# Taps of a causal convolution pinned to their place in the source, and a lighter gate for gated attention, in a one-core decoder layer

## The chip, the cores and the metric

The kernel runs on one core of a Trainium2 chip. The metric is the device time in microseconds of one execution, taken as the median of several. The engines are named as in the profile: PE (TensorE matmul, with PEld for its weight loads), DVE (VectorE), ACT (ScalarE), POOL (GpSimd) and SP (SyncE, which only issues transfers here). Each has its own queue and works through it strictly in order.

## The reference

One layer over 256 tokens of width 2048. The input is projected into four groups of mixers; their outputs are scaled, projected by `w_out`, added and normalized; then comes a mixture of 32 experts and a second normalization. What the change touches lies in the first part:

```python
u = x @ w_in[i]
a_u, gq, gk, gv, g_low, g_r, cq, ck, cv, sb, sc, sh = jnp.split(u, split_idx, axis=-1)
y_a = conformer_conv(a_u, ...)   # h = a * sigmoid(gate); causal depthwise conv of 31 taps; LayerNorm; silu
y_b = gla_mixer(gq, gk, gv, g_low, g_r, w_g2, b_g2, norm_g)
y_c = dilated_mixer(cq, ck, cv, rel_bias)
y_d = short_gated_conv(sb, sc, sh, conv_w)
...
# in gla_mixer, 8 chunks of 32 tokens:
log_a = log_sigmoid(g_low @ w_g2 + b_g2) / 16
b = cumsum(log_a within a chunk)          # then exp(b), exp(b - b_mid), exp(b_last - b) scale q and k
```

## The kernel before

The first 400 us are one long row of projections: eleven blocks of 512 columns of `w_in` (in order cg, ca, v, qk, r, cq, ck, cv, sc, sh, sb) and then `w_out` (wo). Each block has 16 steps, one for 128 rows of the weights. To get float32 accuracy from a faster format, a step splits its weights in two: `split` (L249) lets ACT round them to `wh` (L253), and then DVE or POOL subtracts to get the rest, `wl` (L256). A counter `nsplit` decides which: of three splits in a row, two are DVE's and the third POOL's. PE then does three kinds of matmul for each quarter of the block: `wh` with the rounded input `xh` (L276), `wh` with the input's rest `xl` (L277), `wl` with `xh` (L278); twelve matmuls a step. In the blocks v and cv (L295 to L297) the roles of weights and inputs are swapped and there are six wider matmuls a step. The pool of staged halves has 8 buffers, so four pairs of `wh` and `wl`.

Between the steps `pump` lets generators do the rest of the work in small pieces. `tasks` come first, and `behind` is served only when no task is left. `conv` (L320, in `behind`) computes the 31-tap convolution on DVE: for each of four channel blocks `cb` a first multiplication (L323) and then 30 taps (L325), each adding a shifted, scaled copy of `hp` to `ya`, with a yield after every second tap; then its LayerNorm with sums over PE, and `silu`. `gla_gate` (L398, a task during qk) turns the projected gate into the factors `e12`, `e34` and `dec`; `gla_state` (during r) computes the attention's states, `gla_out` (during cq) its output. `attention` and `sconv` run during sc, sh and sb.

The code gives the data flow; the order in which an engine's queue holds its instructions is chosen by a list scheduler with its own model of durations. It may hold back or bring forward everything that no data ties down. After the first 400 us comes the routing and the mixture of experts, whose order on PE is written out by hand and which the change does not touch.

Of the kernel before, what the change touches and what calls it, by code (L numbers as in the profile page):

```python
# [12 lines left out]
AF = mybir.ActivationFunctionType  # L13
ALU = mybir.AluOpType
# [5 lines left out]
P = 128  # L20
T = 256
# [103 lines left out]
def trunk(ctx, tc, where, vecs_d, lasting, early, gla, xT, x, pT_d, w_in, w_out, ple_w_gate, exp_w_gu, exp_w_down, ple_w_proj, out):  # L125
    nc = tc.nc
    V, S, G, PE = nc.vector, nc.scalar, nc.gpsimd, nc.tensor
# [14 lines left out]
    def bank(name="bank", tag="mx", bufs=None):  # L142
        return pp.tile([P, 512], F32, name=name, tag=tag, bufs=bufs)

    def work(shape, dt=F32, name="w"):
        return wk.tile(shape, dt, name=name, tag="w")

    def stage(shape, dt=F32R, name="st"):
        return st.tile(shape, dt, name=name, tag="st")
# [4 lines left out]
    def f32(ap):  # L154
        return ap.bitcast(F32)
# [8 lines left out]
    def const(name, r=P, t=None):  # L164
        a, n = (at_l if t is None else t)[name]
        return {id(None): cl, id(at_e): ce, id(at_g): cg_}[id(t)][0:r, a:a + n]

    def col(name, i=0):
        a = at_l[name][0] + i
        return cl[:, a:a + 1]  # L170

    def dww(k, cb):
        i = k * 4 + cb
        return const("conf_dw_w", t=at_e)[:, i:i + 1]
# [37 lines left out]
    def quarter(q, part, shape=None, name="mix"):  # L212
        return qm.tile(shape or [P, 4, T], F32 if shape else F32R, name=name, tag=f"q{q}{part}")
# [5 lines left out]
    nsplit = [0]  # L219
    debt = [0]  # L220

    def pump(n=1):

        debt[0] = debt[0] + n if tasks or behind else 0
        while debt[0] >= 1 and (tasks or behind):
            q = tasks or behind
            try:
                next(q[0])
                debt[0] -= 1
            except StopIteration:  # L230
                q.pop(0)
        if not (tasks or behind):
            debt[0] = 0

    def drain():
        while tasks:
            pump()

    def load_half(w, name, sizes=(4, 4), before=None):

        s = slot([P, 8, 512], name)
        a = 0
        for n in sizes:
            if before is not None:
                before(a, a + n)
            nc.sync.dma_start(s[:, a:a + n], w[:, a:a + n])
            a += n
        return s

    def split(w):  # L250
        wh = stage([P, w.shape[1]], F32R, "wh")
        wl = stage([P, w.shape[1]], F32R, "wl")
        S.copy(wh, w)  # L253
        e = G if nsplit[0] % 3 == 2 else V
        nsplit[0] += 1
        e.tensor_sub(wl, w, f32(wh))  # L256
        return wh, wl

    def first_half(k, w, name):
        s = load_half(w, name, (4, 4) if k else (1, 1, 2, 4), lambda a, b: load_x(slice(k + a, k + b)))  # L260
        if k:
            small_loads()
        return s

    def proj_ch(name, rate=1, first=False):

        w = w_in[list(BLOCKS).index(name)]
        bs = [bank(name + "0", "ps"), bank(name + "1", "ps")]
        for k in range(KT):
            if k % 8 == 0:  # L270
                s = first_half(k, w[k // 8], name + "w") if first else load_half(w[k // 8], name + "w")
            wh, wl = split(s[:, k % 8, :])
            for cb in range(4):
                o = bs[cb // 2][:, (cb % 2) * T:(cb % 2 + 1) * T]
                h, l = wh[:, cb * P:(cb + 1) * P], wl[:, cb * P:(cb + 1) * P]
                PE.matmul(o, h, xh[:, k, :], start=(k == 0 and cb % 2 == 0), stop=False, skip_group_check=True)  # L276
                PE.matmul(o, h, xl[:, k, :], start=False, stop=False, skip_group_check=True)  # L277
                PE.matmul(o, l, xh[:, k, :], start=False, stop=(k == KT - 1), skip_group_check=True)  # L278
            pump(rate)
        return [bs[cb // 2][:, (cb % 2) * T:(cb % 2 + 1) * T] for cb in range(4)]  # L280
# [20 lines left out]
    def put_mix(kt, y):  # L301

        q, a = kt // 4, kt % 4
        if (q, "h") not in mix:
            mix[q, "h"], mix[q, "l"] = quarter(q, "h"), quarter(q, "l")
        h = mix[q, "h"][:, a:a + y.shape[1], :]
        S.copy(h, y)
        V.tensor_sub(mix[q, "l"][:, a:a + y.shape[1], :], y, f32(h))
# [7 lines left out]
    hp = quarter(0, "l", [P, 4, T], "hp")  # L316
# [3 lines left out]
    def conv():  # L320
        ya = quarter(3, "h", [P, 4, T], "ya")
        for cb in range(4):
            V.tensor_scalar(ya[:, cb, :], hp[:, cb, :], dww(30, cb), const("conf_dw_b", t=at_e)[:, cb:cb + 1], op0=ALU.mult, op1=ALU.add)  # L323
            for d in range(1, 31):
                V.scalar_tensor_tensor(ya[:, cb, d:T], hp[:, cb, 0:T - d], dww(30 - d, cb), ya[:, cb, d:T],  # L325
                                       op0=ALU.mult, op1=ALU.add)
                if d % 2 == 0:
                    yield
        def total(v):
            u = work([P, 2, T], name="u")  # L330
            V.tensor_add(u, v[:, 0:2], v[:, 2:4])
            V.tensor_add(u[:, 0], u[:, 0], u[:, 1])
            return u[:, 0]

        u = total(ya)
        yield
        b = bank("mu")
        PE.matmul(b[:, 0:T], ones, u, start=True, stop=True)
        V.scalar_tensor_tensor(ya, b[:, None, 0:T].to_broadcast([P, 4, T]), -1.0 / 512, ya, op0=ALU.mult, op1=ALU.add)
        yield  # L340
        sq = work([P, 4, T], name="sq")
        S.activation(sq, ya, AF.Square)
        u = total(sq)
        yield
        b = bank("var")
        PE.matmul(b[:, 0:T], ones, u, start=True, stop=True)
        yield
        rs = work([P, 2, T], name="rs")
        S.activation(rs[:, 0], b[:, 0:T], AF.Sqrt, scale=1.0 / 512, bias=eps_ln[:, 0:1])
        V.reciprocal(rs[:, 1], rs[:, 0])  # L350
        yield
        V.tensor_mul(ya, ya, rs[:, 1:2, :].to_broadcast([P, 4, T]))
        yield
        for cb in range(4):
            S.activation(ya[:, cb, :], ya[:, cb, :], AF.Silu, scale=col("conf_ln_g", cb), bias=col("conf_ln_b", cb))
            V.tensor_scalar_mul(ya[:, cb, :], ya[:, cb, :], col("mix_scale", cb))
            yield
        for cb in range(4):
            put_mix(cb, ya[:, cb:cb + 1, :])
            yield  # L360
# [30 lines left out]
    e12 = work([P, 2, 2, T], name="e12")  # L391
    e34 = work([P, 2, 2, T], name="e34")
# [5 lines left out]
    def gla_gate():  # L398
        zb = bank("z")
        for blk in range(2):  # L400
            PE.matmul(zb[:, blk * T:(blk + 1) * T], const("wg2", P, at_g)[:, blk * P:(blk + 1) * P], glT, start=True, stop=True)
        zz = work([P, 2, 2, T], name="zz")
        z, az = zz[:, 0], zz[:, 1]
        for blk in range(2):
            V.tensor_scalar(z[:, blk, :], zb[:, blk * T:(blk + 1) * T], col("gla_b_g2", blk), None, op0=ALU.add)
        yield
        S.activation(az, z, AF.Abs)
        S.activation(az, az, AF.Exp, scale=-1.0)
        yield
        S.activation(az, az, AF.Ln, bias=1.0)  # L410
        V.tensor_scalar_min(z, z, 0.0)
        V.tensor_sub(az, z, az)
        yield
        cm = work([P, T], name="cm")
        V.memset(cm, 1.0)
        V.memset(cm.rearrange("p (n c) -> p n c", c=32)[:, :, 0:1], 0.0)
        V.tensor_scalar_mul(az, az, 1.0 / 16)
        yield
        bb = z
        for blk in range(2):  # L420
            V.tensor_tensor_scan(bb[:, blk, :], cm, az[:, blk, :], 0.0, ALU.mult, ALU.add)
            yield
        b4 = v4(bb)
        dd = az
        V.tensor_sub(v4(dd), b4, b4[:, :, 16:17].to_broadcast([P, 16, 32]))
        S.activation(e12[:, 0], dd, AF.Exp)
        S.activation(e12[:, 1], dd, AF.Exp, scale=-1.0)
        yield
        V.tensor_sub(v4(e34[:, 1]), b4[:, :, 31:32].to_broadcast([P, 16, 32]), b4)
        S.activation(e34[:, 0], bb, AF.Exp)  # L430
        S.activation(e34[:, 1], e34[:, 1], AF.Exp)
        V.tensor_copy(dec[:, :, None], v4(e34[:, 0])[:, :, 31:32])
        yield

    tasks.append(gla_gate())
    us = proj_ch("qk", 0.6)
    drain()
    ob = []

    def gla_state():  # L440
# [374 lines left out]
    for k2 in range(KT // 2):  # L815
# [6 lines left out]
        for j in range(2):  # L822
# [4 lines left out]
            else:  # L827
                V.tensor_scalar(x1T[:, k, :], b[:, j * T:(j + 1) * T], col("ln1_g", k), col("ln1_b", k),
                                op0=ALU.mult, op1=ALU.add)
# [85 lines left out]
    for q in range(3):  # L915
        V.scalar_tensor_tensor(key, i32[0:32], rk[:, 1:2], const("tab", 32)[:, 32 * q:32 * q + 32], op0=ALU.is_equal,
                               op1=ALU.mult, accum_out=rk[:, 3 + q:4 + q])
# [361 lines left out]
```

## Time and profile before

| | us |
|---|---|
| median of 3 runs | 950.66 (947.5 to 951.43) |
| the profiled execution's own time | 952.04 |
| its span | 950.3 |
| PE busy | 902.4 (95%) |
| DVE busy | 445.1 (47%) |
| ACT busy | 297.0 (31%) |
| POOL busy | 126.9 (13%) |

The shares are means over two very different halves. Up to about 400 us the projections run, with PE busy nearly all the time and DVE, ACT and POOL preparing operands. After that the weights of the experts stream in at about 400 GB/s. The granted clock of PE is at its full level for all of the projections. How far an engine limits the first half is read block by block, from windows cut at the first matmul of each block.

### The profile page before, as it was taken

How to read it: one execution, taken by the hardware profiler on the slowest of the kernel's cores; microseconds unless marked ns; L12 is line 12 of the kernel's file. 1: busy time of each engine (PE TensorE's matmuls, PEld its weight loads, DVE VectorE, ACT ScalarE, POOL GpSimd, SP SyncE). 2: the span in 40 equal slices, each digit the busy share in tenths (PEclk: the TensorE clock that was granted, in tenths of full speed). 3: DMA queues.
4: the chain of work that ended last, by engine and by line, in shares of the span. 5: the costliest groups of instructions: out<-in, count | busy, mean ns of one | idle time of the engine just before them, and what ended most of it. 6: DMA issues, size and time to landing. Idle time of an engine off the chain costs nothing. (4 is left out here: it accounts for less than half of the span.)

```text
span 950.3 us, 14908 instructions
## 1 busy us (share of the span) xinstructions
PE 902.4 (95%) x5550; PEld 549.6 (58%) x5550; DVE 445.1 (47%) x905; ACT 297.0 (31%) x540; POOL 126.9 (13%) x112
## 2 busy tenths in 40 slices
PE   8999899999999999989989999999999999998995
PEld 8987887998989888944333353233533452441221
DVE  4379999746457554574343041022502453340335
ACT  5445523557544544551110021001301221121013
POOL 2232312332313332200000001000000000000000
PEclk9999999999999999989999999999999999999995
DMA  9964423553544754329999999999999999999972
GB/s 353 375 254 159 178 89 118 220 202 127 182 174 167 264 196 178 133 78 370 381 398 410 399 400 413 400 407 413 409 408 396 415 417 416 410 406 393 347 277 91
DMA packets 75535, 280.88 MB, mean 296 GB/s; under 512 B 6904, under 2 KB 7168, under 8 KB 63040
## 3 DMA queue, kind: packets, MB, share of 16 engines
q1 hardware_dynamic: 72256, 269.10, 73.7%
q0 software_dynamic: 2912, 10.50, 2.7%
q8 instruction: 45, 0.74, 0.3%
q10 hardware_dynamic: 288, 0.26, 0.1%
q14 instruction: 34, 0.28, 0.1%
HBM read 290.31 MB, written 2.11 MB: 308 GB/s over the span
## 5 line engine op out<-in xcount | busy, mean ns | idle before, releaser
L1119 PE MATMUL gu<-we,xg 128*32 128x512 f32 x1168 | 146.5, 597 | 5.6 <-DMA we<-in_exp_w_gu_dram 5.6
L747 PE MATMUL pl<-plw,x1T 128*128 128x512 f32 x256 | 123.0, 615 | 0.0
L1164 PE MATMUL y<-wd,hT 128*32 128x512 f32 x624 | 90.9, 599 | 8.4 <-DMA wd<-in_exp_w_down_dram 4.1
L1184 DVE TENSOR_TENSOR acc<-acc,sc 128x512 f32<-128x512 f32 x76 | 50.4, 684 | 95.9 <-PE sc L1182 95.9
L1119 PEld LDWEIGHTS gu<-we,xg 128*32 128x32 f32 x1168 | 34.7, 109 | 98.1 <-issue 73.2
L747 PEld LDWEIGHTS pl<-plw,x1T 128*128 128x128 f32 x256 | 46.5, 192 | 65.7 <-issue 64.7
L1145 DVE SCALAR_TENSOR_TENSOR h<-h,gw,gu 128x256 f32<-128x256 f32 x10 | 4.8, 481 | 166.4 <-ACT h L1144 166.4
L1144 ACT ACTIVATE h<-gu 128x256 f32<-128x256 f32 x10 | 3.8, 385 | 200.7 <-PE gu L1119 200.7
L325 DVE SCALAR_TENSOR_TENSOR ya<-hp,ce,ya 128x255 f32<-128x255 f32 (+29 forms) x120 | 65.4, 591 | 0.2
L1168 ACT CAST yh<-y 128x512 fp32r<-128x512 f32 x40 | 23.5, 587 | 113.4 <-PE sc L1181 68.9
L253 ACT CAST wh<-wow 128x512 fp32r<-128x512 f32 (+1 forms) x80 | 42.8, 535 | 47.4 <-PE wo L296 32.9
L1164 PEld LDWEIGHTS y<-wd,hT 128*32 128x32 f32 x624 | 19.9, 109 | 59.1 <-issue 26.1
L296 PE MATMUL wo<-wh,mix 128*128 128x512 f32 (+1 forms) x160 | 54.1, 347 | 0.0
L295 PE MATMUL wo<-wh,mix 128*128 128x512 f32 (+1 forms) x160 | 54.1, 347 | 0.0
L256 DVE TENSOR_TENSOR wl<-wow,wh 128x512 fp32r<-128x512 f32 (+1 forms) x53 | 31.3, 593 | 43.1 <-ACT wh L253 39.7
L972 PE MATMUL xg<-M,xnh 128*128 128x256 f32 x160 | 44.7, 312 | 3.6 <-ACT xg L977 2.7
L724 POOL DMA_DIRECT2D plw<-in_ple_w_gate_dram x16 | 8.5, 533 | 287.8 <-PE pl L747 180.5
L977 ACT ACTIVATE xg<-xg,cl 128x256 f32<-128x256 f32 x42 | 23.5, 565 | 67.6 <-DVE xg L980 63.6
L297 PE MATMUL wo<-wl,mix 128*128 128x512 f32 (+1 forms) x160 | 42.6, 347 | 0.0
L1169 DVE TENSOR_TENSOR yl<-y,yh 128x512 fp32r<-128x512 f32 x40 | 27.4, 686 | 32.3 <-ACT yh L1168 31.2
L972 PE MATMUL xg<-M,xnl 128*128 128x256 f32 x160 | 40.6, 287 | 0.0
L972 PEld LDWEIGHTS xg<-M,xnh 128*128 128x128 f32 x160 | 31.1, 195 | 14.9 <-issue 7.2
(486 smaller groups left out, 1942.9 us busy)
## 6 DMA issues: line engine op xcount, KB each, us to landing
we<-in_exp_w_gu_dram SPq DMA_DIRECT2D x164, 512.0 KB, 10.2
wd<-in_exp_w_down_dram SPq DMA_DIRECT2D x92, 512.0 KB, 10.8
we<-in_exp_w_gu_dram SPq DMA_DIRECT2D x32, 1024.0 KB, 15.0
wow<-in_w_out_dram SPq DMA_DIRECT2D x16, 1024.0 KB, 7.3
wd<-in_exp_w_down_dram SPq DMA_DIRECT2D x16, 1024.0 KB, 17.1
wd<-in_exp_w_gu_dram SPq DMA_DIRECT2D x24, 512.0 KB, 5.5
plw<-in_ple_w_gate_dram POOLq DMA_DIRECT2D x16, 512.0 KB, 7.0
plw<-in_ple_w_gate_dram SPq DMA_DIRECT2D x6, 1024.0 KB, 6.5
```

The source lines that it names most:

```text
L253: S.copy(wh, w)
L256: e.tensor_sub(wl, w, f32(wh))
L295: PE.matmul(o, lh(k)[:, ts], wh, start=i == 0, stop=False)
L296: PE.matmul(o, ll(k)[:, ts], wh, start=False, stop=False)
L297: PE.matmul(o, lh(k)[:, ts], wl, start=False, stop=i == KT - 1)
L325: V.scalar_tensor_tensor(ya[:, cb, d:T], hp[:, cb, 0:T - d], dww(30 - d, cb), ya[:, cb, d:T], op0=ALU.mult, op1=ALU.add)
L747: PE.matmul(bs[t], x1T[:, k, t * P:(t + 1) * P], s, start=False, stop=k == KT - 1, skip_group_check=True)
L972: PE.matmul(o, part[:, t, (k0 + j) * P:(k0 + j + 1) * P], m_[:, t, :], start=j + t + i == 0, stop=t + i == 2, skip_group_check=True)
L1119: PE.matmul(gu[us, :], xg[:, k0 + k, xo + us.start:xo + us.stop], s[:, q, k, :], start=k0 + k == 0, stop=k0 + k == KT - 1, skip_group_chec ...
L1164: PE.matmul(y[us, :], hT[:, k, us], s[:, q, k, c0:c0 + 512], start=k == 0, stop=k == 1, skip_group_check=True, tile_position=(0, us.start))
L1169: V.tensor_sub(yl, y, f32(yh))
L1184: V.tensor_add(rows(acc, t, db), rows(acc, t, db), o)
```

## The change

Four edits, all in the first half.

- Each tap of the convolution is pinned with `keep_in_program_order`. This adds an edge (order alone, no wait) from the tap to the instruction that the source put just before it on DVE. The first multiplications (L323 before, L325 after) are not pinned.
- `split` gives POOL the remainder 1 in place of 2, and during the block qk every second split in place of every third.
- The gate loses three DVE instructions: the two fills of the mask `cm` become POOL's, and stand ahead of the gate, and the multiplication by 1/16 goes into the scale of the four exponentials on ACT.
- qk is served at a rate of 0.5 pieces a step in place of 0.6.

```diff
     def split(w):
...
-        e = G if nsplit[0] % 3 == 2 else V
+        e = G if nsplit[0] % (2 if halved[0] else 3) == 1 else V
...
             for d in range(1, 31):
-                V.scalar_tensor_tensor(ya[:, cb, d:T], hp[:, cb, 0:T - d], dww(30 - d, cb), ya[:, cb, d:T],
-                                       op0=ALU.mult, op1=ALU.add)
+                tap = V.scalar_tensor_tensor(ya[:, cb, d:T], hp[:, cb, 0:T - d], dww(30 - d, cb), ya[:, cb, d:T],
+                                             op0=ALU.mult, op1=ALU.add)
+
+                tc.keep_in_program_order(tap)
...
-        cm = work([P, T], name="cm")
-        V.memset(cm, 1.0)
-        V.memset(cm.rearrange("p (n c) -> p n c", c=32)[:, :, 0:1], 0.0)
-        V.tensor_scalar_mul(az, az, 1.0 / 16)
-        yield
...
-        S.activation(e12[:, 0], dd, AF.Exp)
-        S.activation(e12[:, 1], dd, AF.Exp, scale=-1.0)
+        S.activation(e12[:, 0], dd, AF.Exp, scale=1.0 / 16)
+        S.activation(e12[:, 1], dd, AF.Exp, scale=-1.0 / 16)
...
-        S.activation(e34[:, 0], bb, AF.Exp)
-        S.activation(e34[:, 1], e34[:, 1], AF.Exp)
+        S.activation(e34[:, 0], bb, AF.Exp, scale=1.0 / 16)
+        S.activation(e34[:, 1], e34[:, 1], AF.Exp, scale=1.0 / 16)
...
+    cm = work([P, T], name="cm")
+    G.memset(cm, 1.0)
+    G.memset(cm.rearrange("p (n c) -> p n c", c=32)[:, :, 0:1], 0.0)
     tasks.append(gla_gate())
-    us = proj_ch("qk", 0.6)
+    halved[0] = True
+    us = proj_ch("qk", 0.5)
     drain()
+    halved[0] = False
```

What this does to the queues is shown at three places. The first is DVE at the start of the block qk. `wl<-qkw` is a split of qk's weights, `ya<-hp` a tap (its length is 256 less its distance, so 128x246 is the tenth), `zz` the gate. Before:

```order
L256 TENSOR_TENSOR wl_920<-qkw_900,wh_919 128x512
L325 SCALAR_TENSOR_TENSOR ya_704<-hp_659,ce_83,ya_704 128x247 x3
L325 SCALAR_TENSOR_TENSOR ya_704<-hp_659,ce_83,ya_704 128x246
L405 TENSOR_SCALAR zz_938<-z_935,cl_81 128x256 x2
L415 MEMSET cm_1026 128x256
L256 TENSOR_TENSOR wl_958<-qkw_900,wh_957 128x512
L325 SCALAR_TENSOR_TENSOR ya_704<-hp_659,ce_83,ya_704 128x246 x3
L325 SCALAR_TENSOR_TENSOR ya_704<-hp_659,ce_83,ya_704 128x245
```

The same place on DVE after (L327 is the tap now, L258 the split):

```order
L258 TENSOR_TENSOR wl_945<-qkw_903,wh_944 128x512
L327 SCALAR_TENSOR_TENSOR ya_704<-hp_659,ce_83,ya_704 128x232
L409 TENSOR_SCALAR zz_941<-z_938,cl_81 128x256 x2
L327 SCALAR_TENSOR_TENSOR ya_704<-hp_659,ce_83,ya_704 128x231
L327 SCALAR_TENSOR_TENSOR ya_704<-hp_659,ce_83,ya_704 128x230
L415 TENSOR_SCALAR zz_941<-zz_941 128x512
L327 SCALAR_TENSOR_TENSOR ya_704<-hp_659,ce_83,ya_704 128x229
L258 TENSOR_TENSOR wl_979<-qkw_903,wh_978 128x512
L327 SCALAR_TENSOR_TENSOR ya_704<-hp_659,ce_83,ya_704 128x228
L327 SCALAR_TENSOR_TENSOR ya_704<-hp_659,ce_83,ya_704 128x227
L416 TENSOR_TENSOR zz_941<-zz_941 128x512
```

Before, four taps of the same distance, one for each channel block, follow each other; after, a channel block's taps follow one another, each adding to what the one before has written. In the whole block qk stand 31 taps and 11 splits before, 13 taps and 8 splits after.

The second place is DVE in the middle of the block ck. Before, it holds splits and the end of the attention's output:

```order
L256 TENSOR_TENSOR wl_1998<-ckw_1919,wh_1997 128x512
L533 TENSOR_TENSOR yb_1614<-oT_1717,sr_1582 128x4x128
L256 TENSOR_TENSOR wl_2036<-ckw_1919,wh_2035 128x512
L308 TENSOR_TENSOR mix_1740<-yb_1614,mix_1739 128x256 x4
L256 TENSOR_TENSOR wl_2054<-ckw_1919,wh_2053 128x512
L256 TENSOR_TENSOR wl_2095<-ckw_2071,wh_2094 128x512
```

After, it holds splits and taps:

```order
L327 SCALAR_TENSOR_TENSOR ya_704<-hp_659,ce_83,ya_704 128x242
L258 TENSOR_TENSOR wl_2130<-ckw_2070,wh_2129 128x512
L327 SCALAR_TENSOR_TENSOR ya_704<-hp_659,ce_83,ya_704 128x241
L327 SCALAR_TENSOR_TENSOR ya_704<-hp_659,ce_83,ya_704 128x240
L258 TENSOR_TENSOR wl_2148<-ckw_2070,wh_2147 128x512
L327 SCALAR_TENSOR_TENSOR ya_704<-hp_659,ce_83,ya_704 128x239
L327 SCALAR_TENSOR_TENSOR ya_704<-hp_659,ce_83,ya_704 128x238
L327 SCALAR_TENSOR_TENSOR ya_704<-hp_659,ce_83,ya_704 128x237
```

Over the blocks the 120 taps stood 30, 31, 38 and 21 in v, qk, r and cq before; they stand 25, 13, 7, 11, 33, 29 and 2 in v, qk, r, cq, ck, cv and sc after. The convolution's LayerNorm, which was in cv, is in sc. The attention's output, which was shared by cq and ck, is all in cq; the eight state updates that stood in cq are in r.

The third place is POOL at the start of qk, after:

```order
L258 TENSOR_TENSOR wl_923<-qkw_903,wh_922 128x512
L436 MEMSET cm_898 128x256
L437 MEMSET cm_898 128x8
L258 TENSOR_TENSOR wl_961<-qkw_903,wh_960 128x512
L258 TENSOR_TENSOR wl_995<-qkw_903,wh_994 128x512
```

Before, POOL had five splits of qk and no fills; after, it has eight splits and the two fills of `cm`.

## Rows read from the trace of the kernel before

**Rows 1.** The page: busy tenths of PE and DVE in 40 slices.
```profile
PE   8999899999999999989989999999999999998995
DVE  4379999746457554574343041022502453340335
```

**Rows 2.** Busy time by block (v, qk, r, cq, ck, cv); columns in the first row.
```profile
core 0: us, PE busy (x) PEld busy (x) DVE busy (x) ACT busy (x) POOL busy (x), PEclk, DMA share, GB/s
59.40:82.70 23.30, 23.15 (x101) 18.41 (x99) 23.30 (x46) 9.38 (x16) 9.28 (x6) 1.00 0.59 220
82.70:110.40 27.70, 23.87 (x188) 22.39 (x187) 27.70 (x54) 16.41 (x25) 7.96 (x5) 1.00 0.40 148
110.40:151.30 40.90, 39.53 (x304) 31.92 (x303) 40.04 (x89) 14.55 (x26) 10.24 (x7) 1.00 0.42 155
151.30:178.60 27.30, 27.30 (x216) 24.73 (x216) 25.20 (x48) 12.16 (x23) 8.72 (x8) 1.00 0.32 112
178.60:201.70 23.10, 23.10 (x197) 23.10 (x197) 10.27 (x19) 12.30 (x26) 7.12 (x6) 1.00 0.63 231
201.70:226.40 24.70, 24.70 (x109) 19.25 (x108) 13.93 (x22) 14.75 (x27) 6.46 (x5) 1.00 0.46 169
```

**Rows 3.** Groups of PE's instructions, 80 to 125 us: busy, mean ns, idle before.
```profile
L278 PE MATMUL qk<-xh,wl 128*128 128x256 f32 x64 | 16.9, 291 | 3.8 <-DVE wl L256 2.2 <-DVE cm L416 1.5
L278 PE MATMUL r<-xh,wl 128*128 128x256 f32 x25 | 6.5, 294 | 1.1 <-DVE wl L256 1.1
```

**Rows 4.** Timeline in qk: start us, us, instruction, idle before and its releaser.
```profile
103.61 1.48 POOL L256 TENSOR_TENSOR wl<-qkw,wh 128x512 fp32r<-128x512 f32 x1 [2.80 <-DMA cqw<-in_w_in_dram]
103.93 1.42 DVE L325 SCALAR_TENSOR_TENSOR ya<-hp,ce,ya 128x242 f32<-128x242 f32 x1
...
104.55 0.27 PE L277 MATMUL qk<-xl,wh 128*128 128x256 f32 x1
105.27 0.68 DVE L256 TENSOR_TENSOR wl<-qkw,wh 128x512 fp32r<-128x512 f32 x1
105.88 0.84 DVE L325 SCALAR_TENSOR_TENSOR ya<-hp,ce,ya 128x242 f32<-128x242 f32 x2
...
106.01 0.39 PE L278 MATMUL qk<-xh,wl 128*128 128x256 f32 x1 [1.18 <-DVE wl L256]
...
106.64 0.68 DVE L256 TENSOR_TENSOR wl<-qkw,wh 128x512 fp32r<-128x512 f32 x1
```

**Rows 5.** Timeline of DVE in the routing: L959 reads what L958 writes.
```profile
423.95 0.35 DVE L958 TENSOR_SCALAR M<-cl,rel 128x256 f32<-128x256 f32 x1
424.34 0.48 DVE L959 SCALAR_TENSOR_TENSOR M<-cl,rel,M 128x256 fp32r<-128x256 f32 x1
424.75 0.35 DVE L958 TENSOR_SCALAR M<-cl,rel 128x256 f32<-128x256 f32 x1
```

**Rows 6.** Timeline where PE comes to qk: the first split, and who waits for it.
```profile
83.68 0.68 DVE L256 TENSOR_TENSOR wl<-qkw,wh 128x512 fp32r<-128x512 f32 x1
...
84.42 0.39 PE L278 MATMUL qk<-xh,wl 128*128 128x256 f32 x1 [0.59 <-DVE wl L256]
```

**Rows 7.** Timeline of ACT in the gate: from the absolute value to the logarithm.
```profile
88.49 0.64 ACT L407 ACTIVATE zz<-zz 128x512 f32<-128x512 f32 x1 [2.31 <-DVE zz L405]
...
93.39 0.63 ACT L410 ACTIVATE zz<-zz 128x512 f32<-128x512 f32 x1
```

**Rows 8.** Groups of DVE's instructions, 62 to 110 us: taps, and two that the change removes.
```profile
L325 DVE SCALAR_TENSOR_TENSOR ya<-hp,ce,ya 128x255 f32<-128x255 f32 (+15 forms) x61 | 34.5, 616 | 0.0
...
L417 DVE TENSOR_SCALAR zz<-zz 128x512 f32<-128x512 f32 x1 | 0.4, 419 | 0.0
...
L415 DVE MEMSET cm<- 128x256 f32 x1 | 0.3, 272 | 0.0
```

**Rows 9.** Timeline around the start of cv: its first split, and that split's first use.
```profile
198.19 0.69 DVE L256 TENSOR_TENSOR wl<-cvw,wh 128x512 fp32r<-128x512 f32 x1 [0.67 <-ACT wh L253]
...
202.17 0.39 PE L297 MATMUL cv<-wl,xh 128*128 128x512 f32 x1
```

More of the change, by code (lines that the diff above doesn't have):

```diff
@@ L248, in load_half @@
         return s
+    halved = [False]
     def split(w):
```

## The prediction

> **What bounds the kernel now.** First the page's slices [rows 1]: PE is near full in all of the first half, where the change lies, and DVE is full in slices 4 to 7, the blocks v to r. So I cut the windows at the blocks [rows 2]. PE is the bound wherever it gets its operands: ck takes 23.10 us for 197 matmuls, 0.117 us each, 1.41 us for a step of twelve. The block qk has 194 (192 of its own, two of the gate; the trace has 188 of them) and should take 22.75; it takes 27.70. So 4.95 us are lost there, in a block where DVE is busy for all of the 27.70. The waits name the same pair: matmuls with `wl` wait for the split on DVE [rows 3]. Idle time there adds to 3.8 us in qk and 1.1 in r; counted from start to start (104.55 to 106.01 where 0.12 is the rule [rows 4]) it is more. With r's two stalls, 1.3 and 0.4, and 0.3 at the end of v the shortage of DVE costs about 6.9 us. That is all the change can win: in the other blocks PE is full, and DVE there is 44 to 92% busy.
>
> Why DVE is short is in the timeline [rows 4]. A tap takes 0.38 from start to start (two in 0.76), a split 0.61. But the tap that begins at 103.93, while POOL does a split, holds DVE for 1.34: about 1.0 more. It is the rule, not a chance: the 61 taps between 62 and 110 us have a mean of 0.616 [rows 8] where an undisturbed one lasts 0.46, 9.5 us too much, and POOL did nine splits there. I reckon 1.0 for each POOL split wherever DVE has no pause. So a split on POOL takes 0.6 from DVE and gives 1.0 back. Bare (splits at 0.60, taps at 0.37 to 0.39 by their length, the rest by the trace's own start-to-start times) DVE's work before is 6.0 + 11.8 + 3.0 = 20.8 us in v, 6.6 + 11.9 + 4.1 = 22.6 in qk, 6.6 + 14.3 + 11.9 = 32.8 in r; with five, four and five collisions 25.8, 26.6, 37.8, against 23.3, 22.75 and about 39 of PE. DVE starts v some 4 us ahead, has lost that lead when qk begins [rows 6], and lags through qk.
>
> **The change part by part.** *The gate.* Removed from DVE are the fill (0.2 to 0.3) and the multiplication (0.33) [rows 8]; the tiny second fill counts nothing. The scale inside ACT's exponentials costs nothing, the instruction is there already. The fills on POOL lie in its pauses: 7.96 of 27.70 busy [rows 2]. Gain on DVE: 0.6 us.
>
> *Half of qk's splits on POOL.* Three splits less, 1.8 us off DVE; eight collisions in place of four, 4.0 more. By itself this loses 2.2 us of DVE's time.
> The Trainium skill (SBUF — State Buffer, "Who interferes with whom") says that DVE and GpSimd share one pair of ports as an exclusive lock, and that an operation with two SBUF inputs on DVE waits out a GpSimd operation that reads SBUF; it speaks against this part, and the rows above agree.
>
> *The taps.* In qk 18 fewer: 6.9 us off. But a channel block's taps now follow each other, and each needs the one before. Such a pair is in the trace elsewhere [rows 5]: L959 reads L958's output and starts 0.39 after it, though L958 lasts 0.35, a gap of 0.04. The next, which depends on nothing, starts 0.07 before L959 ends, and taps overlap by 0.08 in the same way. So a dependent neighbour costs 0.115 us. In the new order about 44 taps stand directly behind the tap they need (9 in v, 6 in qk, 13 in ck, 11 in cv): 5 us more DVE work in all.
> The Trainium skill (VectorE: DVE Perf Modes, "The DRAIN you can't avoid") says that a semaphore between two DVE operations costs nothing extra; the rows above do not bear it out. By that rule this term is zero, which is the third rival.
>
> Sum for DVE by block after, bare (splits + taps + rest) + dependent neighbours + collisions, against PE:
> v 6.6 + 9.7 + 3.0, + 1.0 + 5.0 = 25.3, PE 23.3.
> qk 4.8 + 4.9 + 3.8, + 0.7 + 8.0 = 22.2, PE 22.75.
> r, with all state updates and seven taps, about 29, PE 39.
> cq 6.6 + 4.2 + 8.5, + 0.2 + 5.0 = 24.5, PE 23.6 (192 matmuls and eight transposes).
> ck 6.6 + 12.6 + 0, + 1.5 + 5.0 = 25.7, PE 22.5.
> cv 6.0 + 10.9 + 0, + 1.3 + 6.0 = 24.2, PE 22.5 (the attention's matmuls move on to sc).
> sc, with the LayerNorm, 17 + 5 = 22, PE about 24.
>
> In place of one block far over (qk) there are three a little over. What that costs depends on DVE's lead. With an idle DVE it is 3.3 us: cv's first split ends at 198.88 and is used at 202.17 [rows 9].
>
> *Entry and qk, step by step.* Before, qk's first split starts at 83.68 [rows 6]. Ahead of it now stand one more split (+0.6), five taps fewer (-1.9), nine dependent neighbours (+1.0), perhaps half a collision less (-0.5): it ends at 83.5, and PE wants it at 82.9. Stall 0.6. After that PE needs a DVE split every second step, 2.82 us. Until the second one stand four taps (1.85), the split (0.6), a collision (1.0): 3.45, stall 0.6. Until the third three taps and two more behind the gate's operations, 1.6, these operations 1.1, split and collision 1.6: 4.3, stall 1.5. Then L416 waits for ACT's logarithm, which is done 5.5 us after the gate's first step [rows 7] (88.49 to 94.02), at about 93.8 here, where DVE would be there at 92.2; with what follows, stall 1.6. Then two scans, a subtraction and split with collision, 3.5: stall 0.7. Behind that DVE has hardly any taps left and gets ahead. Together 5.0 us, for 6.9 before: the block as a whole fits, but its work lies at the front. In r DVE has 10 us to spare, so its stalls shrink to those for the first `kk` and states, about 0.5. Gain: 1.4 us.
>
> *cq, ck, cv, sc.* DVE comes out of r with its lead of 3.3. It loses 0.9 in cq, 3.2 in ck and 1.7 in cv: 5.8, that is 2.5 us more than the lead. PE waits for these 2.5 us. In sc the sums of the LayerNorm go DVE, PE, DVE, ACT, DVE, with splits queued behind each; in cv they cost nothing because DVE was half idle (13.93 of 24.70 [rows 2]). With no lead left, PE reaches the first sum 2.4 us into sc and DVE has 2.6 to 3.6 us ahead of it: I take 1.0. Bounds of ck to sc: 0, if two of the collisions a block fall on pauses, and 7, if the lead out of cq is gone (the attention's output there waits on ACT and PE) and both LayerNorm sums wait.
>
> Everything later keeps its order on PE, and the experts' transfers can't begin before the routing, so a microsecond lost or won in the first half is one at the end. Net: -1.4 + 2.5 + 1.0 = +2.1 us. The sum is made against the profiled execution's 952.04 (span 950.3 and 1.7 around it), which is 1.4 above the median of 950.66; on the median I get 952.7 and write 952.5.
>
> **The rivals.**
> *DVE starves PE from ck to sc.* The upper bounds above hold, 7 us, and qk keeps 5.5 of its stalls: +6 or more, 956 to 959. For it: ck and cv have 92 and 81% of PE's time in bare and dependent work alone, and qk's 4.95 us in the trace are what 117% with collisions looks like; ck would be at 114%. Against: the lead, which qk did not have. It decides from a lead out of cq below about 1 us.
> *The stalls simply go.* If the collisions are fewer where the taps are spread, qk stalls by some 2 and ck to sc by none: -5 to -6, 945 to 946. For it: DVE's bare load in no block exceeds 92% of PE's time any longer. Against: the collisions of rows 4, which recur with nearly every POOL split when DVE is dense.
> *Dependent neighbours cost nothing* (as the page has it). Then v and qk are shorter by 1.7 us, ck and cv by 2.8: no loss in cv, qk's stalls about 3.5, net -2.5: 948.
> *It does not do what it says.* The pin ties a tap to one neighbour only; the first taps of the channel blocks still move ahead (they do, in v). This would leave taps where they were; the new queue shows them moved, so I give it nothing.
>
> **How the numbers follow.** A difference under 0.5%, 4.75 us, is about what a measurement of this kernel can't tell from none. Forecast and third rival both lie within it: 0.48 and 0.15. Starving above 955.4: 0.20. Stalls gone below 945.9: 0.17. That gives faster 0.17, same 0.63, slower 0.20. The range of 8 in 10 goes from 945, which takes in half of the second rival, to 957.5, which takes in the lower half of the first; the forecast's own runs from 949.5 to 955.4.
>
> **What would show it.** In the changed profile: qk's window at 26 to 28 us in place of 27.70, with waits of L278's matmuls for DVE's splits in its first half only; r at about 39.5; ck and cv together 2 to 3 us longer than PE's 45, with DVE full and matmuls waiting for DVE; taps in ck with gaps of +0.03 between them where before they overlap; a tap or split of 1.3 us and more at each POOL split. The prediction is wrong if ck and cv show no wait at all (collisions or dependent neighbours cost less than I took), or if qk's stalls are gone (its front-loaded order does not matter), or if r grows (the states' chain was too tight).

## The result: slower by 0.8%

| | median us (runs) | profiled execution: own time, span |
|---|---|---|
| before | 948.19 (947.50 to 951.43, 5) | 952.04, 950.3 |
| after | 957.54 (955.54 to 959.39, 5) | 958.11, 956.3 |

The ratio is 1.0081, 95% interval 1.0066 to 1.0096: about 7.7 us, more than the half per cent that counted as no change. (The medians of the five runs each lie 9.4 apart, the two profiled executions 6.1.) The forecast of 952.5 is missed by 5 us, at the edge of the range (957.5); what came is the first rival, DVE starving PE from ck to sc. That the time lies about at the range's end is owed to this rival, for which the range had been widened, and not to the forecast's sum.

The windows of the changed kernel, cut at the first matmul of each block from v to sb, answer [rows 2]:

```profile
core 0: us, PE busy (x) PEld busy (x) DVE busy (x) ACT busy (x) POOL busy (x), PEclk, DMA share, GB/s
58.63:81.99 23.36, 23.36 (x102) 18.88 (x101) 23.04 (x41) 9.58 (x16) 8.43 (x7) 1.00 0.61 228
81.99:110.51 28.52, 25.06 (x193) 23.32 (x192) 19.18 (x33) 17.63 (x28) 12.25 (x9) 1.00 0.45 165
110.51:154.29 43.78, 43.78 (x314) 33.24 (x313) 24.41 (x59) 12.23 (x21) 7.69 (x6) 1.00 0.34 129
154.29:176.94 22.65, 22.65 (x195) 22.65 (x193) 20.18 (x40) 13.25 (x26) 8.30 (x7) 1.00 0.41 144
176.94:202.14 25.20, 24.64 (x203) 23.89 (x202) 24.74 (x41) 11.71 (x23) 8.68 (x6) 1.00 0.45 168
202.14:226.72 24.58, 23.39 (x96) 17.16 (x95) 24.19 (x43) 10.57 (x19) 8.27 (x6) 1.00 0.48 175
226.72:254.62 27.90, 26.09 (x205) 24.40 (x204) 21.91 (x43) 20.00 (x40) 8.50 (x6) 1.00 0.40 147
...
284.52:314.55 30.03, 29.87 (x232) 26.90 (x231) 21.76 (x51) 13.75 (x31) 7.81 (x6) 1.00 0.50 178
```

DVE is full in ck and cv now (24.74 of 25.20, 24.19 of 24.58), no longer in qk (19.18 of 28.52). From v's first matmul to wo's first it is 255.92 us; before it was 249.3 (59.4 to 308.7). From there to the end both take the same, 641.7 and 641.6; v begins 0.8 earlier than before. So the loss of 6.6 us lies between v and sb. A block's length alone misleads, since the small matmuls of attention and LayerNorm also moved from one block to another (cv had twelve of them and has none). What PE lost is therefore counted from the start of each of a projection's matmuls to the start of the next matmul, as the excess over the block's usual pitch (0.118 us, in v and cv 0.235); of the small matmuls only their waits count:

| us lost by PE in | v | qk | r | cq | ck | cv | sc | sh | sb | sum |
|---|---|---|---|---|---|---|---|---|---|---|
| before | 0.7 | 5.4 | 4.2 | 1.0 | 0.1 | 0.5 | 0.4 | 1.1 | 1.5 | 14.9 |
| after | 0.3 | 5.8 | 4.8 | 0.2 | 1.6 | 2.6 | 4.1 | 0.6 | 1.5 | 21.4 |

The difference, 6.5, is the 6.6 of the windows: ck, cv and sc lose 7.3 more, the other blocks 0.8 less. The waits of PE from 55 to 316 us say for whom, to be read beside [rows 3]:

```profile
engine line waited for: us in total, times, longest us
PE qk L280 <- DVE wl L258: 1.7, 3, 0.7
PE qk L280 <- POOL wl L258: 1.4, 2, 0.7
PE cv L299 <- DVE wl L258: 1.0, 3, 0.5
PE pt L605 <- DVE sc__2623 L603: 0.7, 1, 0.7
PE ck L280 <- DVE wl L258: 0.5, 1, 0.5
PE sc L280 <- DVE wl L258: 0.5, 1, 0.5
PE sc L278 <- ACT wh L255: 0.4, 1, 0.4
PE mu L342 <- DVE u L336: 0.2, 1, 0.2
```

Before, all of PE's waits for DVE lay in qk and r, but for one in sb. Now there are waits in ck, cv and sc, and in qk two matmuls wait for POOL's own split.

How DVE falls behind is in its timeline in ck, to be read beside [rows 4]:

```profile
start us, us, engine line op out<-in xcount [idle before <-releaser]
186.04 0.68 DVE L258 TENSOR_TENSOR wl<-ckw,wh 128x512 fp32r<-128x512 f32 x1
186.64 2.00 DVE L327 SCALAR_TENSOR_TENSOR ya<-hp,ce,ya 128x250 f32<-128x250 f32 x4
188.56 0.68 DVE L258 TENSOR_TENSOR wl<-ckw,wh 128x512 fp32r<-128x512 f32 x1
189.16 1.51 DVE L327 SCALAR_TENSOR_TENSOR ya<-hp,ce,ya 128x246 f32<-128x246 f32 x1
190.59 0.68 DVE L258 TENSOR_TENSOR wl<-ckw,wh 128x512 fp32r<-128x512 f32 x1
```

There is not one pause. Four taps that each wait for the one before take 2.00; the next, beside a POOL split, takes 1.51 alone. From 186.04 to 190.59 that is two DVE splits and one on POOL, so three steps of PE at 1.41: 4.55 of DVE's time against 4.23 of PE's.

### The profile page after: what moved, and what is told of

The parts are those of the page before. It is cut to its first block, busy times and chain, and to the rows that moved or that the text cites. A ratio compares the mean times of both kernels' runs of the same rounds, so it can differ in the third digit from the quotient of the medians.

```text
span 956.3 us, 14899 instructions
## 1 busy us (share of the span) xinstructions
PE 908.5 (95%) x5550; PEld 549.6 (57%) x5550; DVE 450.7 (47%) x899; ACT 297.1 (31%) x540; POOL 133.1 (14%) x117
## 5 line engine op out<-in xcount | busy, mean ns | idle before, releaser
L327 DVE SCALAR_TENSOR_TENSOR ya<-hp,ce,ya 128x249 f32<-128x249 f32 (+21 forms) x120 | 70.8, 605 | 1.7
L258 DVE TENSOR_TENSOR wl<-wow,wh 128x512 fp32r<-128x512 f32 (+1 forms) x54 | 31.3, 585 | 45.3 <-ACT wh L255 44.3
```

Of the source, the lines that this page charges most:

```text
L327: tap = V.scalar_tensor_tensor(ya[:, cb, d:T], hp[:, cb, 0:T - d], dww(30 - d, cb), ya[:, cb, d:T], op0=ALU.mult, op1=ALU.add)
```

## Experiments

Every ratio is to the kernel before, run beside it; 0.1% is 0.95 us. Losses of PE are counted as in the table above.

**Which edit.** The pin alone, on the kernel before:

```diff
-                V.scalar_tensor_tensor(ya[:, cb, d:T], ...)
+                tap = V.scalar_tensor_tensor(ya[:, cb, d:T], ...)
+                tc.keep_in_program_order(tap)
```

> The kernel before with nothing changed but the pinned taps; the splits, the gate and the rate of qk stay. In its queue of DVE the taps stand 24, 14, 8, 10, 30 and 34 in v, qk, r, cq, ck and cv (25, 13, 7, 11, 33 and 29 with all four edits, 30, 31, 38 and 21 in v to cq before). Theory A: the pin alone makes the loss, because it puts more than half of the taps into ck and cv, where DVE then needs more time than PE. By it ck to sc lose about 7 us as with all four edits; qk has three more splits on DVE and four collisions with POOL fewer, so it is 0 to 2 us shorter. Time 4 to 10 us above the kernel before. Theory B: the loss comes from the other edits (every second split of qk on POOL, the other remainder of the count, the rate). By it this kernel is within 2 us of the kernel before or faster.

Measured: 1.0072 (1.0048 to 1.0096). PE loses 7.2 us from ck to sc (1.0 before, 8.3 with all edits) and 4.4 in qk. Theory A holds: the pin by itself makes nearly all of the loss.

All edits but the pin:

```diff
-                tc.keep_in_program_order(tap)
```

> All edits but the pin: the scheduler places the taps freely. They stand 32, 36, 36 and 16 in v, qk, r and cq, none in ck and cv, much as before; qk has 8 splits on DVE in place of 11, and 8 on POOL in place of 5. Theory A: nothing is lost from ck to sc. In qk DVE's bare work is 4.8 of splits, 13.7 of taps and 3.8 of the gate, 22.3 us, and eight collisions of 1.0 make it 30.3, against 26.6 by the same count before: qk stalls 2 to 4 us more than before. Time 0 to 4 us above the kernel before. Theory B (the other edits make the loss): 7 to 10 us above. If collisions cost little, qk is shorter than before, and the time 1 to 3 us below it.

Measured: 1.0006 (0.9990 to 1.0022), no difference. From ck to sc no more is lost than before. In qk it is 8.5 against 5.4, as the eight collisions let one expect, though one wait of 1.0 us in it is for a split of POOL's own; r and sb give 2.1 back (2.9 for 4.2, 0.7 for 1.5).

All four edits, but with every third split of qk on POOL, not every second:

```diff
-    halved[0] = True
     us = proj_ch("qk", 0.5)
```

> All four edits but one: in qk every third split goes to POOL, as in the other blocks, and not every second. The queue of DVE is the same but for three more splits in qk (11 in place of 8); taps stay at 25, 13, 7, 11, 33, 29 and 2. If a POOL split beside a dense DVE takes about 1.0 us from DVE and gives 0.6 back, qk's stalls (5.8 us with all four edits) fall by about 1.2, and the time is 0 to 2 us below that with all four edits, so 5 to 8 us above the kernel before. If POOL's splits relieve DVE, as their count alone would have it, qk's stalls grow by 1.8 us. From ck to sc nothing changes in either case: about 8 us of stalls.

Measured: 1.0055 (1.0036 to 1.0074). With the same taps at the same places qk loses 3.6 us in place of 5.8. So moving three splits to POOL costs PE 2.2 us in qk; it does not relieve DVE where that counts. (The time alone would not show it, since its interval overlaps with that of the change.) From ck to sc nothing changed (8.3). The waits for splits in qk are now

```profile
PE qk L280 <- DVE wl L258: 1.1, 1, 1.1
...
PE qk L280 <- POOL wl L258: 0.3, 1, 0.3
```

where the change has 1.7 and 1.4: more of the difference lies in waits for POOL's own splits than in waits for DVE's.

**Dependent neighbours and place.** The taps in another order, all else as in the change:

```diff
         for cb in range(4):
             V.tensor_scalar(ya[:, cb, :], hp[:, cb, :], ...)
-            for d in range(1, 31):
+        for d in range(1, 31):
+            for cb in range(4):
                 tap = V.scalar_tensor_tensor(...)
                 tc.keep_in_program_order(tap)
-                if d % 2 == 0:
+                if cb % 2 == 1:
                     yield
```

> All four edits, but the source's order of the taps is changed: the distance is the outer loop and the channel block the inner one, so a tap's neighbour belongs to another channel block and does not wait for it. The sums are the same. Pinned like this the taps stand 32, 2, 8, 12, 41 and 25 in v to cv, none in sc. Theory A has three parts that this kernel pulls apart. With 2 taps in qk DVE has 4.8 + 0.8 + 3.8 + 8 of collisions = 17.4 us of work there: the stalls of qk (5.8) should fall below 2. If dependent neighbours cost 0.115 us each, ck and cv lose 24 x 0.115 = 2.8 us of DVE work, which leaves 48.4 us against PE's 45 and a lead of up to 3.3: ck to sc lose 0 to 3 us, not 9; time 1 to 5 us above the kernel before or level with it. If dependent neighbours cost nothing, ck to sc lose as much as with all four edits as they stand (9 us of stalls), and only qk gains: 3 to 6 us above.

Measured: 1.0072 (1.0051 to 1.0093), outside both expectations. The price of a dependent neighbour is plain in the trace; four taps in ck now take

```profile
192.25 1.58 DVE L328 SCALAR_TENSOR_TENSOR ya<-hp,ce,ya 128x236 f32<-128x236 f32 x4
```

against 2.00 in the changed kernel: 0.42 less for three such neighbours, of which some 0.06 are the shorter taps. That is 0.12 each, the 0.115 of the forecast. But it brought no time: ck and cv hold 66 taps in place of 62, and they lose 6.9 us (4.2 in the changed kernel), sc 1.6. And qk, with two taps in it, still loses 4.9, because v is overfull with 32 and the first split of qk comes 2.2 us late. What follows on that stall is in the windows around it:

```profile
core 0: us, PE busy (x) PEld busy (x) DVE busy (x) ACT busy (x) POOL busy (x), PEclk, DMA share, GB/s
81.60:83.90 2.30, 0.40 (x2) 0.00 (x0) 2.30 (x4) 1.20 (x3) 1.60 (x4) 1.00 0.87 285
83.90:87.80 3.90, 3.78 (x19) 3.78 (x20) 2.57 (x6) 2.39 (x3) 0.00 (x0) 0.57 0.85 357
87.80:98.00 10.20, 10.20 (x87) 10.10 (x86) 5.65 (x8) 8.72 (x15) 2.66 (x2) 1.00 0.34 119
```

PE idles for 2 us, and then the granted clock is 0.57 for 3.9 us, mostly its lower level (1.2 GHz of 2.4), with a matmul every 0.213 us: a further 1.7 us, on top of the 2.2 of the stall itself.

The same, with the block r served faster, so that taps move from ck and cv into r and cq:

```diff
-    rb = proj_ch("r", 1.15)
+    rb = proj_ch("r", 2.0)
```

> As the kernel with interleaved, pinned taps, but the block r is served at a rate of 2.0 pieces a step in place of 1.15, so that the convolution goes on in r, where DVE has time left. Taps stand 32, 2, 26, 22 and 38 in v, qk, r, cq and ck, none in cv; the LayerNorm of the convolution is back in cv. Theory A (what costs is taps and LayerNorm late, in blocks where DVE needs more than PE's time): cv and sc lose nothing, ck is the only dense block left (DVE 6.6 + 14.3 + 5 and the end of the attention's output, against 22.5), with a lead to spend; qk stalls below 2. Time 1 to 5 us below the kernel before. If the place of the taps does not matter and their number of collisions does, it is level with the kernel of interleaved taps at the old rate.

Measured: 1.0058 (1.0036 to 1.0079); the expected gain did not come. What theory A says of cv and sc holds (0.5 and 0.9 lost), but the loss has only moved: ck loses 6.9, 2.9 in one wait and about 2 more at the lower clock after it. With 22 taps in cq DVE comes to ck without a lead and with 38 taps to do.

**POOL's splits.** The kernel before, with the splits of v, qk and r all on DVE (`dense[0]` is true during these blocks):

```diff
-        e = G if nsplit[0] % 3 == 2 else V
+        e = G if nsplit[0] % 3 == 2 and not dense[0] else V
```

> The kernel before, with every split of the blocks v, qk and r on DVE and none on POOL (16 each on DVE in place of 10, 11 and 11); the taps float as before and stand at 25, 26, 33, 26 and 10 in v to ck. Theory: what starves PE in qk before is the hold that a POOL split puts on DVE, 1.0 us each against the 0.6 that DVE needs for the split itself. By it DVE's work is 9.6 + 9.5 + 3.0 = 22.1 us in v (25.8 before), 9.6 + 9.9 + 4.1 = 23.6 in qk (26.6) and 34 in r (37.8): qk's stalls fall from 5.4 to under 2.5 and r's large ones go; time 3 to 5 us below the kernel before. Rival: DVE is simply short of time, and 16 more splits (9.6 us) make it worse: qk's stalls grow by 3 and more; time 2 to 5 us above.

Measured: 0.9966 (0.9948 to 0.9984). DVE has 16 splits more to do, and the kernel is faster:

```profile
core 0: us, PE busy (x) PEld busy (x) DVE busy (x) ACT busy (x) POOL busy (x), PEclk, DMA share, GB/s
57.40:78.90 21.50, 21.50 (x95) 17.36 (x93) 21.50 (x50) 8.78 (x15) 0.00 (x0) 1.00 0.65 247
78.90:101.14 22.24, 22.24 (x182) 21.87 (x180) 19.60 (x44) 14.56 (x23) 0.58 (x1) 1.00 0.46 176
```

qk takes 22.24 us, with nothing lost. So the stalls that the change set out to remove came from the hold of POOL's splits on DVE, and not from too many splits on DVE. Part of it may be that the scheduler put five taps fewer into qk (26 for 31), about 1.9 us of DVE at 0.38 each; the change without POOL, further down, has no such help. The Trainium skill (SBUF — State Buffer, "Who interferes with whom") has a DVE instruction with two SBUF inputs contend with a GpSimd instruction that reads SBUF. This run agrees: four taps in qk lasted 1.42 us and more before, none here lasts over 0.9, and the 5.4 us are gone.

The same cure where the change hurts: all four edits, and the splits of ck, cv and sc on DVE (`dense[0]` is true there):

```diff
-        e = G if nsplit[0] % (2 if halved[0] else 3) == 1 else V
+        e = G if nsplit[0] % (2 if halved[0] else 3) == 1 and not dense[0] else V
```

> All four edits, and every split of the blocks ck, cv and sc on DVE, none on POOL there (16 each in place of 11, 10 and 11). Taps stand at 25, 13, 7, 11, 25, 28 and 11 in v to sc. If collisions with POOL are what makes these blocks too long for DVE, its work is 9.6 + 9.4 + 1.2 = 20.2 us in ck and 9.6 + 10.6 + 1.3 = 21.5 in cv, under PE's 22.5, and the stalls in ck and cv (1.6 and 2.6 us) go; what is left is the late LayerNorm in sc, with more taps ahead of it; time 2 to 5 us below that with all four edits, 2 to 6 above the kernel before. If the collisions cost nothing here, the extra splits (9.6 us over three blocks) lengthen ck to sc by 5 us and more.

Measured: 1.0044 (1.0026 to 1.0062). ck and cv lose nothing any more, sc 0.3 in place of 4.1. (ck has five splits more there and eight taps fewer, 25 for 33.) Some is given back behind: one wait of 2.3 us for ACT in sh, where the `silu` of the late LayerNorm and the attention's softmax come together on ACT and the weights are not rounded in time, and 1.8 us in wo, into which 14 matmuls of the attention now reach.

The kernel before, with v, qk and r free of POOL's splits, and the lighter gate of the change:

```diff
-        V.tensor_scalar_mul(az, az, 1.0 / 16)
...
-        S.activation(e12[:, 0], dd, AF.Exp)
+        S.activation(e12[:, 0], dd, AF.Exp, scale=1.0 / 16)
...
+    G.memset(cm, 1.0)
```

> The kernel before, with every split of v, qk and r on DVE, and the gate made lighter as in the change (fills of the mask on POOL, 1/16 in the exponentials), nothing pinned, rate 0.6. If the gate's three operations are worth the 0.6 us of DVE that they take there, and DVE bounds qk, this is 0.3 to 0.8 us below the same kernel with the gate as it was; if they lie under other work, level with it. Against the kernel before 3 to 6 us below if the hold of POOL's splits is what counts, 2 to 5 above if DVE is simply short of time.

Measured: 0.9940 (0.9921 to 0.9960). That is 0.3% below the run without the lighter gate, but the two intervals overlap: in the expected direction, not shown.

**No split on POOL at all**, with floating taps and the lighter gate:

```diff
-        e = G if nsplit[0] % 3 == 2 and not dense[0] else V
+        e = V
```

> The kernel before with the lighter gate, floating taps, and no split on POOL in any block. Taps stand at 26, 26, 31, 23 and 14 in v to ck. Against the kernel that keeps POOL out of v, qk and r alone, DVE has five or six more splits in each of the later blocks, 3.0 to 3.6 us, and no hold by POOL. Theory (a POOL split takes 1.0 from a dense DVE and gives 0.6 back, and nothing where DVE has pauses): cq and ck are the only other blocks where DVE is dense, and they had no stalls to lose; so level with it, 4 to 7 us below the kernel before. If POOL's splits are worth something where DVE has pauses, sc to wo stall and it is 1 to 4 us slower than that kernel.

Measured: 0.9931 (0.9915 to 0.9947); from 55 to 316 us the trace names no wait of PE any more.

The change as it stands, without POOL:

```diff
-        e = G if nsplit[0] % (2 if halved[0] else 3) == 1 else V
+        e = V
```

> All four edits (taps pinned, channel block by channel block), and no split on POOL in any block. Taps stand at 19, 19, 5, 10, 25, 30 and 12 in v to sc. What is left of the pin's price is then dependent neighbours (0.115 us each) and the late place: DVE's work is 9.6 + 7.4 + 3 + 0.7 = 20.7 us in v, 9.6 + 7.4 + 4 + 0.7 = 21.7 in qk, 20.6 in ck and 22.6 in cv, all within PE's time. If collisions are the larger part of the loss, the stalls from qk to cv (10 us with all four edits) go to under 3, and what remains is the late LayerNorm and attention, which now reach into wo: 2 us below to 3 above the kernel before. If the pin itself is the larger part, it stays 4 us and more above.

Measured: 0.9975 (0.9963 to 0.9987). From 1.0081 to here is what POOL's splits cost the change, about 1%. In qk, ck and cv it loses 0.1 in all, although qk now holds 19 taps and 16 splits on DVE, where the change has 13 and 8: with POOL out of the way, more work on DVE starves PE less. Against floating taps (0.9931) the pinned order still costs 0.4%. The trace shows 3.5 us from v's first matmul to wo's last (331.9 against 328.4): r and cq lose 5.1 us against 3.0, sh has a wait of 1.4 for ACT, and wo now holds 14 matmuls of the attention.

The same edit on the kernel with interleaved taps and r at 2.0:

> All four edits, the taps interleaved over the channel blocks and pinned, r served at 2.0 pieces a step, and no split on POOL in any block. Taps stand at 26, 8, 24, 24, 26 and 12 in v to cv, the LayerNorm at the end of cv and in sc. With no collisions and no dependent neighbours only the fixed place of the taps is left of the change. DVE's work: 9.6 + 9.8 + 3 = 22.4 us in v, under 18 in qk, 9.6 + 9.1 + 8.5 = 27.2 in cq (a lead of 3.3 to spend), 22 in ck. Theory: stalls of cq and ck under 2 us, 2 to 6 us below the kernel before. If a fixed place costs by itself (the scheduler can't move a split ahead), 0 to 3 us above.

Measured: 0.9921 (0.9906 to 0.9936), 940.74 us: the lowest median of all, ahead of both kernels; its interval overlaps with that of floating taps (0.9931). So a pin is no loss by itself, if its place leaves no block overfull.

And between these two, the same with r at its old rate:

```diff
-    rb = proj_ch("r", 2.0)
+    rb = proj_ch("r", 1.15)
```

> All four edits, the taps interleaved over the channel blocks and pinned, no split on POOL in any block, r at its old rate of 1.15 pieces a step. It stands between two kernels that have run: with the taps channel block by channel block it was at 0.9975 of the kernel before, with interleaved taps and r at 2.0 pieces at 0.9921. Taps stand at 26, 8, 8, 12, 30, 29 and 7 in v to sc. If what is left of the pin's price is the late place (LayerNorm and attention pushed back, into wo), it is level with the first, 0.996 to 1.000; if it is the dependent neighbours, level with the second, 0.991 to 0.994.

Measured: 0.9956 (0.9942 to 0.9970), level with neither. Its interval lies apart from that of the faster rate: what the rate does counts, 0.35%. In the trace that is 1.9 us in r, where the states' matmuls are less scattered (2.4 lost, not 4.3), and 14 matmuls of the attention that stay out of wo. It overlaps with that of the dependent taps: what dependent neighbours cost in time, once DVE has room, stays open.

## Why the forecast went wrong, step by step

**What bounds the kernel: right in place, one step short in kind.** DVE did starve PE, and POOL's hold (1.0 us a split) was seen. In ck and cv of the changed kernel, where DVE has no pause, the eleven POOL splits hold DVE for 5.2 and 6.3 us, as forecast (5.0 and 6.0). But the forecast took the hold for one term among several. It was the term: without POOL's splits no block is overfull, before or after.

**Half of qk's splits on POOL: the number right, by luck.** Forecast: 2.2 us of DVE's time lost. Measured by the third experiment: 2.2 us of PE's. But the eight POOL splits of qk hold DVE's taps, scans and splits for about 3.0 us in all, where the forecast's sum has 8.0, and the five of the third experiment for 2.3; DVE is not full there (19.18 of 28.52), so a POOL split often meets no DVE instruction that it could hold. Of the 2.2 us some 1.1 are waits for POOL's own splits, a cost that the forecast did not have.

**Entry and qk: right in size (5.0 forecast, 5.8 measured), partly by another cause.** L416 did make DVE wait for the logarithm, as forecast. But the stall at the entry (0.6) did not come, and of the 5.8, counted from start to start, only some 2.4 us are waits for DVE; 1.7 are for POOL's own splits, 0.6 for ACT's rounding, the rest steps of 0.1. That two matmuls would wait for POOL's own split was not in the forecast:

```profile
90.68 1.28 ACT L414 ACT_TABLE_LOAD   x1
90.74 1.27 POOL L258 TENSOR_TENSOR wl<-qkw,wh 128x512 fp32r<-128x512 f32 x1 [6.72 <-ACT wh L255]
91.98 0.63 ACT L414 ACTIVATE zz<-zz 128x512 f32<-128x512 f32 x1
92.07 0.39 PE L280 MATMUL qk<-xh,wl 128*128 128x256 f32 x1 [0.73 <-POOL wl L258]
92.64 0.69 DVE L416 TENSOR_TENSOR zz<-zz 128x512 f32<-128x512 f32 x1 [2.58 <-ACT zz L414]
```

ACT rounds `wh` late, between table loads for the gate, and POOL then needs twice as long as DVE would. In these rows DVE stands idle for 2.58 us while PE waits for POOL.

**r: the gain was there and was given back.** The two stalls of r went, 1.7 us. But r grew, from 40.9 us to 43.8, which the forecast had named as a sign of being wrong. The cause was not the one named there, too tight a chain of the states, since no wait of PE is left in r. Eight state updates more are in r, each in pieces between r's own matmuls, and each change of stream costs PE about 0.1 us on the way in and again on the way out:

```profile
133.99 0.28 PE L280 MATMUL r<-xh,wl 128*128 128x256 f32 x1
134.20 0.62 PE L506 MATMUL ob<-state,qq 128*32 128x256 f32 x2
134.75 0.39 PE L278 MATMUL r<-xh,wh 128*128 128x256 f32 x1
134.97 0.28 PE L279 MATMUL r<-xl,wh 128*128 128x256 f32 x1
135.09 0.28 PE L280 MATMUL r<-xh,wl 128*128 128x256 f32 x1
```

From 133.99 to 134.20 and from 134.75 to 134.97 it is 0.21 and 0.22 where 0.12 is the rule. There are 49 such steps in r (25 before) and 2 in cq (10). Together r and cq win only 0.2 us, with v and qk level (6.1 both times); 1.4 were forecast for qk's entry, qk and r.

**cq, ck, cv, sc: the step that failed.** Forecast: 3.5 us (2.5 in ck and cv, 1.0 in sc). Measured: 7.3, the upper bound that the forecast gave for it: 3.6 more than before in ck and cv, 3.7 more in sc. Two sizes were off. First the lead with which DVE comes to ck. By the forecast's sum it is 2.4 us (3.3 out of r less 0.9 lost in cq); it is 1.7:

```profile
176.00 0.69 DVE L258 TENSOR_TENSOR wl<-ckw,wh 128x512 fp32r<-128x512 f32 x1
...
178.36 0.28 PE L280 MATMUL ck<-xh,wl 128*128 128x256 f32 x1
```

POOL's hold did not take it: DVE came to cq with 4.9 us (the first split of cq ends at 149.62 and is used at 154.53), and POOL's splits held it for 2.5 there and not for 5.0. The lead went into DVE's own waits in cq, from 148.9 to 176.7 us, for ACT and PE in the attention's output:

```profile
DVE sr L522 <- ACT sr L518: 2.5, 1, 2.5
DVE ss L532 <- ACT ss L531: 1.7, 1, 1.7
DVE yb L538 <- PE oT L537: 0.6, 1, 0.6
```

The forecast knew this wait, but had it in its upper bound alone; in the sum it stood at nothing. With a lead of 1.7 the sum gives 3.2 us for ck and cv. The first rival was to decide from a lead below about 1 us; at 1.7 it already did.

Second, and larger, sc. The late LayerNorm meets not DVE alone but the start of the attention, on ACT and DVE:

```profile
247.31 1.28 ACT L596 ACT_TABLE_LOAD   x1
...
250.37 1.12 ACT L255 CAST wh<-scw 128x512 fp32r<-128x512 f32 x2
250.50 0.18 DVE L599 RECIPROCAL mm<-mm 128x4 f32<-128x4 f32 x1 [1.91 <-ACT sc__2623 L596]
...
251.18 1.58 DVE L603 TENSOR_SCALAR sc__2623<-sc__2623,mm 128x256 f32<-128x256 f32 x2
...
252.81 0.33 PE L605 MATMUL pt<-cl,sc__2623 128*128 128x128 f32 x1 [0.72 <-DVE sc__2623 L603]
```

ACT goes from `silu` to the softmax with a table load, and rounds the next weights only at 250.37; DVE, held by a POOL split, needs 1.58 for two small scalings. PE loses 0.5 and 0.9 there. Another 0.7 at sc's first split is DVE's lag out of cv, and 0.4 is a wait for the LayerNorm's first sum.

**Dependent neighbours: right in price (0.12 against 0.115), not shown to matter.** The third rival, that they cost nothing, falls. The Trainium skill's sentence (VectorE: DVE Perf Modes, "The DRAIN you can't avoid") that a semaphore costs nothing extra is given for a chain of eight copies; for these taps it does not hold, by the 0.12 us above.

**The chances.** The first rival had 0.20, with all the arithmetic for it on the page: ck at 114% of PE's time beside qk's 117%, which had lost 5 us. Only the lead spoke against it, and the lead was assumed from a place in the kernel before where DVE had been idle. No difference was the wrong likeliest case.

What stays open: from wo's first matmul to the end it took 639 to 648 us in the profiled executions of the experiments, and not all of the time won before wo shows in the medians. The kernels without POOL's splits come from v to wo in 239 to 240 us, 9 to 11 less than before, and win 2.4 to 7.5 us in the end. Part of it is work pushed into wo; the rest was not followed up.

## What to carry to other kernels

Count what a helper engine takes from the busy one, not only what it takes over: here a split on POOL saved DVE 0.6 us and held it for 1.0 where DVE had no pause, and more of that made things worse. With none at all the kernel was 0.7 to 0.8% faster than before in the best two forms (floating taps with the lighter gate, and interleaved, pinned taps with r served faster). A pinned order moves work as a floating one does; sum the load of every block it fills, up to the work that it pushes out at the end, before believing the relief in the block that it empties. And a lead is to be read where it is spent, not where the engine was last idle, with the waits that stand between the two.

## What the runs showed of the hardware

- Where DVE had no pause, a POOL split (128x512, two inputs) held one DVE tap or split for about 1.0 us: eleven of them in ck and cv of the changed kernel for 11.5 us. The eight in qk, where DVE stood idle for 9.3 of 28.5 us, held it for about 3.0 in all.
- Three stalls of PE, of 2.2, 2.2 and 2.9 us (in the two kernels with interleaved taps and POOL's splits), were followed by a fall of its granted clock (0.57, 0.64 and 0.71 over the next 3.9 us) and matmuls every 0.213 us in place of 0.118, its lower level. Two others, of 2.2 us in qk without the pin and of 2.5 in sh with POOL kept out of ck to sc, left it at 1.00. What tells them apart was not tried; where the clock falls, a stall of 2 us costs nearly double.
- A change between a projection's matmuls and others, and the first matmul after a wait, cost PE about 0.1 us each (0.21 to 0.22 from start to start in place of 0.12); 63 such steps from v to cq in the changed kernel make about 6 us (43 before).
